# A modulation product moved ahead, a norm's chain put at another priority, and four loads on another queue, in a two-block fp32 kernel

## The chip, the cores and the metric

One Trainium2 chip, one core of it. The metric is the device time of one execution in microseconds (us); before the change three runs gave 2356.71, 2358.75 and 2363.08, median 2358.75. TensorE is called PE, VectorE DVE, ScalarE ACT, GpSimd POOL and the queue of SyncE SP.

## The reference, cut to what matters

Two transformer-like blocks run one after the other on 256 tokens of width 2048, all in fp32.

```python
mod = silu_c @ w_mod[l] + b_mod[l]                       # 2048 -> 6 x 2048
sh1, sc1, g1, sh2, sc2, g2 = split(mod, 6)
hx = modulate(rms_norm(x, norm1_g[l]), sh1, sc1)         # h*(1+scale)+shift
out_x, _, _ = token_mixer(hx, ...)                       # w_in, a scan over tokens, w_pa, w_pb, w_o
x = x + g1 * out_x
h = modulate(rms_norm(x, norm2_g[l]), sh2, sc2)          # the second norm
a, b = split(h @ w_up, 2)
x = x + g2 * ((silu(dwconv_grid(a, dw, db)) * b) @ w_down)   # 3x3 depthwise convolution
# second block: norm, w_in_2, two kinds of attention (one with a per-head norm and rotary
# embedding of q and k, and a norm of its output), gates, w_out_2
```

## The kernel before, in words

Every large product is made on PE in three fp32r parts. A weight block (`blocks`, L138 on) is 512 KB: a DMA on SP's queue into `raw`, ACT makes its rounded part `whi` (L156), DVE the rest `wlo = raw - whi` (L157), and PE uses both. `raw`, `whi` and `wlo` have four buffers each, so the chain SP, ACT, DVE runs up to four blocks ahead of PE. 680 blocks go through it: w_in (from 0), w_pb and w_pa between, w_o (block 224), w_up (256), w_down (320), w_up, w_down, w_up, w_down, w_in_2 (520), w_out_2 (648).

The other work is written as generators. `pump()` (L100) is called after each block and advances the list `bg` (convolution, scans, attention) by one or more yields, and `late`, the generator `late_mod`, by `late_rate` steps. `late_mod` (L655) computes the four parts of `mod` that are needed late: 16 groups of 512 columns, 8 steps each; a step loads 512 KB of w_mod by POOL's queue (L663) into a tile `lm` and adds its two rows of weights to a sum with two DVE instructions (L697; the first of a group L700). With 0.42 steps per pump it ends in the middle of the up-projections.

A scheduler then orders the instructions of each engine by priority, which is the order of writing; what stands under `high_priority(offset=400)` (`AHEAD`, as L156 and L157 do) goes ahead of up to 400 others. Each engine runs its list strictly in order. An instruction in `keep_in_program_order` (`pin`) keeps its place as written.

Around the second norm: `rest` ends with w_o in four column groups; `add_rows` (L1097) adds gate times product to `x`, ACT squares it (L1095), and the last lines make `r2`, the factor of each token. `ffn` scales `x` by `r2` on ACT (L1115), transposes it on PE (L265), and ACT (L1125) and DVE (L1126, L1128) modulate and split it. `x` is loaded by SP's queue in four DMAs of 512 KB just ahead of w_o (L1068). `up(n)` makes 512 columns of a, then of b; `conv` takes 3 of 4 channel groups' taps on DVE (L1166) and the fourth on POOL (L1160, L1162). In the second block `qk_norm` (L1515) and `diff` (L1615) multiply by factors that POOL's queue copies to all partitions (L336), in two pinned halves.

Of the kernel before, what the change touches and what calls it, by code (L numbers as in the profile page):

```python
# [9 lines left out]
AF = mybir.ActivationFunctionType  # L10
ALU = mybir.AluOpType

D = 2048
# [4 lines left out]
EPS = 1e-6  # L18
AHEAD = 400
# [59 lines left out]
class Build:  # L79
    def __init__(self, tc, nc, I, out):  # L80
        self.tc, self.nc, self.I, self.out = tc, nc, I, out
        self.bg = []
        self.late = None
        self.late_rate = 0.42
        self.late_due = 0.0
        self.n_mod = 0
        self.n_name = 0
        self.n_raw = 4
        self.ready = set()
        self.early_cols = (1024, 2048, 2560)  # L90
# [434 lines left out]
        nc.vector.tensor_tensor(out=B, in0=res[1], in1=col(V_BMOD + k0), op=ALU.add)  # L525
        out += [A, B]

    def load_rows(self, ap, i, h):
        t = self.t4((128, 1024))
        self.nc.sync.dma_start(out=t, in_=ap[i * 128:(i + 1) * 128, h * 1024:(h + 1) * 1024])  # L530
        return t

    def norm1(self):
# [434 lines left out]
    def rest(self):  # L968
        nc, v = self.nc, self.vec
        W = self.I["w_in"][0]  # L970
        ax = [self.act(0, i * 128, i * 128 + 128) for i in range(2)]
        tt, stt = nc.vector.tensor_tensor, nc.vector.scalar_tensor_tensor

        def product(c0, out=None, func=AF.Copy):
            banks = self.gemm_tf(W, 0, 16, c0, ax)
            out = self.t4((128, 2, 512))
            for i in range(2):
                nc.scalar.activation(out=out[:, i, :], in_=banks[i], func=func)
            if func is AF.Sigmoid and self.bg:
                self.exp_ln()  # L980
            return out, banks

        def times(banks, o):
            for i in range(2):
                tt(out=o[:, i, :], in0=banks[i], in1=o[:, i, :], op=ALU.mult)

        def conv(g, x, cv):
            u = self.t4((128, 4, 258))
            nc.gpsimd.memset(u[:, :, 0:258:257], 0.0)
            yield  # L990

# [24 lines left out]
        for g in range(2):  # L1016
            x, _ = product(6144 + 512 * g)
            times(self.gemm_tf(W, 0, 16, 7168 + 512 * g, ax), x)
            cv = self.t4()
            self.bg.insert(0, conv(g, x, cv))  # L1020
            x, _ = product(5120 + 512 * g)
            yb.append(self.hl())
            self.bg.insert(0, branch(x, cv, yb[-1]))
        ayb = self.halves(yb)
        mb = []
        for n in range(4):
            sg, _ = product(10240 + 512 * n, func=AF.Sigmoid)
            times(self.gemm_tf(self.I["w_pb"][0], 0, 8, 512 * n, ayb), sg)
            mb.append(sg)

        def attn(sg, g, y):
            on = self.on[g]
            yield

            def fn(b, ps):
                o = on[:, 2 * b:2 * b + 2, :]
                stt(out=o, in0=o, scalar=v[:, V_AN:V_AN + 1], in1=ps, op0=ALU.mult, op1=ALU.mult)
                self.parts(o, y[b])

            yield from self.turned(lambda i: sg[:, i, :], fn)  # L1040
            self.ready.add(y[0].name)

        ya = []
        for g in range(2):
            sg, banks = product(4096 + 512 * g, func=AF.Sigmoid)
            times(banks, sg)
            ya.append(self.hl())
            self.bg.append(attn(sg, g, ya[-1]))
        aya = self.halves(ya)

        def merge(x, y):
            yield
            yield

            def fn(b, ps):
                self.parts(ps, y[b])

            yield from self.turned(lambda i: x[:, i, :], fn)
            self.ready.add(y[0].name)

        mg = []
        for n in range(4):
            sg, _ = product(8192 + 512 * n, func=AF.Sigmoid)
            times(self.gemm_tf(self.I["w_pa"][0], 0, 8, 512 * n, aya), sg)
            tt(out=sg, in0=sg, in1=mb[n], op=ALU.add)
            mg.append(self.hl())
            self.bg.append(merge(sg, mg[-1]))
        self.x = [[self.load_rows(self.I["x"][0], i, h) for h in range(2)] for i in range(2)]  # L1068
        amg = self.halves(mg)
        while self.n_mod < 8:  # L1070
            self.pump()

        self.A2 = self.pc.tile([128, 16], F32, name="A2")
        nc.vector.tensor_scalar(out=self.A2, in0=self.mod[:, 16:32], scalar1=1.0, scalar2=None, op0=ALU.add)
        nc.vector.tensor_tensor(out=self.A2, in0=self.A2, in1=v[:, V_N2:V_N2 + 16], op=ALU.mult)
        ss = self.s1((128, 2, 4))
        for n in range(4):
            banks = self.gemm_tf(self.I["w_o"][0], 0, 16, 512 * n, amg)
            if n == 3:
                self.tc.keep_in_program_order(nc.scalar.preload_act_table_set("natural_log_exp_and_others"))  # L1080
            while self.n_mod < 9 + n:
                self.pump()
            self.add_rows(n, banks, self.gate_rows[0])
            for i in range(2):
                self.squares(self.chunk(i, n), ss[:, i, n:n + 1])
        tot = self.s1((128, 2))
        nc.vector.tensor_reduce(out=tot, in_=ss, axis=mybir.AxisListType.X, op=ALU.add)
        self.r2 = self.s1((128, 2))
        self.rsqrt_mean(self.r2, tot, D, EPS)

    def chunk(self, i, n):
        return self.x[i][n // 2][:, (n % 2) * 512:(n % 2) * 512 + 512]
# [1 line left out]
    def squares(self, x, out):  # L1094
        self.nc.scalar.activation(out=self.t2(), in_=x, func=AF.Square, accum_out=out)  # L1095

    def add_rows(self, n, banks, rows):  # L1097

        nc = self.nc
        r = rows[n // 2][:, (n % 2) * 512:(n % 2) * 512 + 512]  # L1100
        for i, b in enumerate(banks):
            t, x = self.t2(), self.chunk(i, n)
            nc.vector.tensor_tensor(out=t, in0=b, in1=r, op=ALU.mult)
            nc.vector.tensor_tensor(out=x, in0=x, in1=t, op=ALU.add)

    def ffn(self):
        nc, v = self.nc, self.vec
        stt = nc.vector.scalar_tensor_tensor
        hs = [self.hl() for _ in range(4)]

        def normed():
            for n in range(4):
                xs = self.t4((128, 2, 512))
                for i in range(2):
                    nc.scalar.activation(out=xs[:, i, :], in_=self.chunk(i, n), func=AF.Copy,  # L1115
                                         scale=self.r2[:, i:i + 1])
                hf = self.t4()

                def fn(b, ps):
# [16 lines left out]
        n_made = [0]  # L1136

        def wait(k):
            while n_made[0] < min(4, k // 4 + 2):
                next(made, None)  # L1140
                n_made[0] += 1

# [40 lines left out]
        def up(n):  # L1183
            W = self.I["w_up"][0]
            acc = self.t4()
            pads = []
# [12 lines left out]

            self.gemm_wide(W, 0, 16, 512 * n, ah, take, at_once=2 if n else 4, n_pump=1 + n // 8)  # L1200
            y, b = self.hl(), []
            self.bg.append(conv(n, acc, pads, b, y))
            b.append(self.gemm_wide(W, 0, 16, FF + 512 * n, ah, n_pump=2))
            return y

        def down(n0, ys, last):
# [289 lines left out]
    def qk_norm(self, x, wcol, t0):  # L1496

        nc = self.nc
        n = x.shape[2]
# [13 lines left out]
        for i in range(2):  # L1513
            h = slice(2 * i, 2 * i + 2)
            self.pin(nc.vector.scalar_tensor_tensor(out=x[:, h, :], in0=x[:, h, :], scalar=w, in1=rb[:, h, :],  # L1515
                                                    op0=ALU.mult, op1=ALU.mult))
            yield

        for b in (0, 64):
            nc.gpsimd.dma_start(out=rot[b:b + 8], in_=x[b + 8:b + 16])  # L1520
# [18 lines left out]
    def diff(self, g, q, k, vv, do):  # L1539

        nc = self.nc
# [71 lines left out]
        for i in range(2):  # L1613
            h = slice(2 * i, 2 * i + 2)
            self.pin(nc.vector.tensor_tensor(out=do[:, h, :], in0=do[:, h, :], in1=rb[:, h, :], op=ALU.mult))  # L1615
            yield


_INS = [
# [22 lines left out]
```

## Time and profile before

| | |
|---|---|
| median of three runs | 2358.75 us |
| profiled execution, its own time | 2357.4 us |
| its span in the trace | 2355.7 us |
| PE busy, DVE, ACT, POOL | 2279.4 (97%), 1677.1 (71%), 1103.2 (47%), 377.0 us (16%) |
| DMA | 476.19 MB, mean 202 GB/s |
| mean granted PE clock | 0.992 of full speed |

Busy time says how long an engine had an instruction; a line of the waits says which engine stood idle, for whom and how long. Times in stretches are counted from the start of the span.

### The profile page before, as it was taken

The page shows a single profiled execution, that of the slowest core. Times are in us where ns is not written, and L with a number is a line of the kernel's source. Part 1 is how long each engine was busy: PE and PEld are TensorE (multiplying, and loading weights), DVE is VectorE, ACT ScalarE, POOL GpSimd, SP SyncE. Part 2 cuts the span into 40 slices and gives each one's busy share as a digit, 9 for nine tenths or more (in the row PEclk, how much of TensorE's full clock was granted, in tenths as well). Part 3 has the DMA queues.
Part 4 walks back from the last instruction along what each step waited for, and adds up shares of the span by engine and source line. Part 5 has one row for each costly group of instructions (what it writes and reads, how often), then busy time and mean ns, then how long its engine had stood idle before and what let it go on. Part 6 is the DMA issues. An engine that isn't in the chain of part 4 may idle for free. (4 is left out here: it accounts for less than half of the span.)

```text
span 2355.7 us, 33863 instructions
## 1 busy us (share of the span) xinstructions
PE 2279.4 (97%) x12872; PEld 1933.8 (82%) x12872; DVE 1677.1 (71%) x2445; ACT 1103.2 (47%) x1514; POOL 377.0 (16%) x630
## 2 busy tenths in 40 slices
PE   5999999999999999989989999999999999999999
PEld 3689898888888787878777888888888988888887
DVE  3556488788988876888997688757877665653564
ACT  3324344544555543454443445434555463554543
POOL 0200000100001101003540043202220212211000
PEclk9999999999999999999999999999999999999999
DMA  9774443777778778757666666655655657664454
GB/s 317 270 246 158 136 125 120 248 232 240 241 231 269 242 254 315 241 180 232 216 228 214 192 187 184 195 193 186 196 194 183 177 153 162 167 151 126 132 196 155
DMA packets 293123, 476.19 MB, mean 202 GB/s; under 512 B 16153, under 2 KB 151816, under 8 KB 292960
## 3 DMA queue, kind: packets, MB, share of 16 engines
q1 hardware_dynamic: 267120, 387.50, 51.5%
q0 software_dynamic: 25168, 85.50, 12.6%
q8 instruction: 101, 1.65, 0.3%
q10 hardware_dynamic: 672, 1.03, 0.1%
q14 instruction: 62, 0.51, 0.1%
HBM read 468.05 MB, written 2.10 MB: 200 GB/s over the span
## 5 line engine op out<-in xcount | busy, mean ns | idle before, releaser
L156 ACT ACTIVATE whi<-raw 128x1024 fp32r<-128x1024 f32 x680 | 715.7, 1058 | 885.5 <-PE ps L241 399.4
L157 DVE TENSOR_TENSOR wlo<-raw,whi 128x1024 fp32r<-128x1024 f32 x680 | 840.4, 1242 | 364.2 <-ACT whi L156 360.1
L296 PE MATMUL ps<-t,whi 128*128 128x512 f32 (+2 forms) x4096 | 813.4, 343 | 9.1 <-ACT whi L156 5.7
L296 PEld LDWEIGHTS ps<-t,whi 128*128 128x128 f32 x4096 | 633.8, 190 | 108.0 <-issue 26.4
L239 PE MATMUL ps<-whi,t 128*128 128x512 f32 x1376 | 545.3, 396 | 4.2 <-ACT whi L156 4.2
L240 PE MATMUL ps<-wlo,t 128*128 128x512 f32 x1376 | 538.3, 391 | 1.9 <-DVE wlo L157 1.9
L241 PE MATMUL ps<-whi,t 128*128 128x512 f32 x1376 | 538.0, 391 | 0.0
L296 PE MATMUL ps<-t,wlo 128*128 128x256 f32 (+1 forms) x3072 | 441.6, 284 | 18.2 <-DVE wlo L157 18.2
L296 PEld LDWEIGHTS ps<-t,wlo 128*128 128x128 f32 x3072 | 416.2, 190 | 46.6 <-DVE wlo L157 24.1
L239 PEld LDWEIGHTS ps<-whi,t 128*128 128x128 f32 x1376 | 259.4, 189 | 58.8 <-ACT whi L156 4.6
L240 PEld LDWEIGHTS ps<-wlo,t 128*128 128x128 f32 x1376 | 259.5, 189 | 55.3 <-DVE wlo L157 2.7
L241 PEld LDWEIGHTS ps<-whi,t 128*128 128x128 f32 x1376 | 259.3, 188 | 54.2
L663 POOL DMA_DIRECT2D lm<-in_w_mod x128 | 92.8, 725 | 692.7 <-DVE t L697 352.8
L697 DVE SCALAR_TENSOR_TENSOR t<-lm,silc,t 128x512 f32<-128x512 f32 x240 | 180.5, 752 | 5.2 <-DMA lm<-in_w_mod 3.0
L1160 POOL TENSOR_SCALAR cb<-pad,vec 128x256 f32<-128x256 f32 x88 | 84.7, 977 | 430.3 <-DVE pad L211 430.3
L1166 DVE SCALAR_TENSOR_TENSOR t<-pad,vec,t 128x256 f32<-128x256 f32 x264 | 143.6, 573 | 4.3 <-ACT t L1196 2.5
L1162 POOL TENSOR_TENSOR t<-t,cb 128x256 f32<-128x256 f32 x88 | 84.5, 961 | 3.0
L649 DVE TENSOR_TENSOR t<-ps,t 128x256 f32<-128x256 f32 x96 | 36.1, 418 | 57.7 <-PE ps L296 57.6
L296 PE MATMUL ps<-t,t 128*128 128x128 f32 (+5 forms) x352 | 59.1, 332 | 0.8 <-ACT t L1590 0.6
L296 PE MATMUL ps<-em,cstat 128*32 128x512 f32 (+1 forms) x320 | 44.5, 555 | 14.7 <-DVE t L303 11.4
L296 PEld LDWEIGHTS ps<-t,t 128*128 128x128 f32 (+3 forms) x352 | 44.9, 185 | 11.7 <-issue 3.8
L882 ACT ACTIVATE t<-t 128x1024 f32<-128x1024 f32 x28 | 29.6, 1057 | 41.4 <-DVE t L880 36.8
(278 smaller groups left out, 1373.9 us busy)
## 6 DMA issues: line engine op xcount, KB each, us to landing
raw<-in_w_in SPq DMA_DIRECT2D x299, 512.0 KB, 4.1
raw<-in_w_up SPq DMA_DIRECT2D x176, 512.0 KB, 4.0
lm<-in_w_mod POOLq DMA_DIRECT2D x128, 512.0 KB, 5.5
raw<-in_w_down SPq DMA_DIRECT2D x88, 512.0 KB, 3.7
em<-in_w_mod SPq DMA_DIRECT2D x64, 512.0 KB, 6.2
raw<-in_w_o SPq DMA_DIRECT2D x32, 512.0 KB, 4.3
raw<-in_w_out SPq DMA_DIRECT2D x32, 512.0 KB, 3.6
raw<-in_w_in POOLq DMA_DIRECT2D x21, 512.0 KB, 5.8
```

The source lines that it names most:

```text
L156: a = nc.scalar.activation(out=hi, in_=raw, func=AF.Copy)
L157: b = nc.vector.tensor_tensor(out=lo, in0=raw, in1=hi.bitcast(F32), op=ALU.subtract)
L239: nc.tensor.matmul(b, lhsT=ah(kt + k), rhs=hi[:, k, :], start=first, stop=False)
L240: nc.tensor.matmul(b, lhsT=ah(kt + k), rhs=lo[:, k, :], start=False, stop=False)
L241: nc.tensor.matmul(b, lhsT=al(kt + k), rhs=hi[:, k, :], start=False, stop=last)
L296: self.nc.tensor.matmul(o, lhsT=l, rhs=r, start=start, stop=stop, skip_group_check=True)
L649: nc.vector.tensor_tensor(out=e, in0=o, in1=e, op=ALU.add)
L663: nc.gpsimd.dma_start(out=raw, in_=W[kb * 256:kb * 256 + 256, 2 * D + b * 512:2 * D + b * 512 + 512].rearrange("(k p) f -> p k f", p=128))
L697: nc.vector.scalar_tensor_tensor(out=acc, in0=raw[:, j, :], scalar=s, in1=acc, op0=ALU.mult, op1=ALU.add)
L1160: nc.gpsimd.tensor_scalar(out=cb, in0=tap(j, t), scalar1=wt(t, 4 * n + j), scalar2=1.0, op0=ALU.mult, op1=ALU.mult)
L1162: nc.gpsimd.tensor_tensor(out=a, in0=a, in1=cb, op=ALU.add)
L1166: stt(out=a, in0=tap(j, t), scalar=wt(t, 4 * n + j), in1=a, op0=ALU.mult, op1=ALU.add)
```

## The change

`late_rate` is 0.8 until `rest` begins and 0.45 from there. The four loads of `x` go to POOL's queue, one after each of four column groups ahead of w_o. The last column group of w_o is added, squared and reduced under high priority, one half of the tokens after the other. The scaling by `r2` is written ahead of everything else of `ffn`: the first of four chunks half by DVE and half by ACT, at high priority, the other three by POOL. `wait` asks for a normed chunk two k-tiles ahead of its use instead of four. For n below 8 the convolution of `up(n)` is appended to `bg` after b's product instead of ahead of it. In `qk_norm` and `diff` the second pinned half follows five and eight yields after the first instead of one.

```diff
-        self.late_rate = 0.42
+        self.late_rate = 0.8
...
     def rest(self):
+        self.late_rate = 0.45
...
+            self.x[n % 2][n // 2] = self.load_rows(self.I["x"][0], n % 2, n // 2, nc.gpsimd)
-        self.x = [[self.load_rows(self.I["x"][0], i, h) for h in range(2)] for i in range(2)]
...
-            self.add_rows(n, banks, self.gate_rows[0])
-            for i in range(2):
+            if n < 3:
+                self.add_rows(n, banks, self.gate_rows[0])
+                for i in range(2):
+                    self.squares(self.chunk(i, n), ss[:, i, n:n + 1])
+        with self.tc.high_priority(offset=AHEAD):
+            for i in range(2):
+                self.add_rows(n, banks, self.gate_rows[0], (i,))
                 self.squares(self.chunk(i, n), ss[:, i, n:n + 1])
+            nc.vector.tensor_reduce(out=tot, in_=ss, axis=mybir.AxisListType.X, op=ALU.add)
+            self.rsqrt_mean(self.r2, tot, D, EPS)
...
+                if n:
+                    nc.gpsimd.tensor_scalar(out=xs[:, i, :], in0=self.chunk(i, n), scalar1=r, scalar2=1.0,
+                                            op0=ALU.mult, op1=ALU.mult)
+                elif i:
+                    with self.tc.high_priority(offset=AHEAD):
+                        nc.scalar.activation(out=xs[:, i, :], in_=self.chunk(i, n), func=AF.Copy, scale=r)
+                else:
+                    with self.tc.high_priority(offset=AHEAD):
+                        nc.vector.tensor_scalar(out=xs[:, i, :], in0=self.chunk(i, n), scalar1=r, scalar2=None,
+                                                op0=ALU.mult)
...
-            while n_made[0] < min(4, k // 4 + 2):
+            while n_made[0] < min(4, (k + 2) // 4 + 1):
...
-            self.bg.append(conv(n, acc, pads, b, y))
+            work = conv(n, acc, pads, b, y)
+            if n >= 8:
+                self.bg.append(work)
             b.append(self.gemm_wide(W, 0, 16, FF + 512 * n, ah, n_pump=2))
+            if n < 8:
+                self.bg.append(work)
...
-            yield
+            for _ in range(5 - 4 * i):     # qk_norm
+                yield
...
-            yield
+            for _ in range(8 - 7 * i):     # diff
+                yield
```

What DVE does between two weight blocks early in the third up-projection, before and then now (`lm` is a step's load of w_mod, `pad` a plane of the convolution, `ps` a result of PE; lines of the new code are some 20 higher, so that L1186 is the old L1166):

```order
L157 TENSOR_TENSOR wlo_10357<-raw_10354,whi_10356 128x1024
L697 SCALAR_TENSOR_TENSOR t_1706_10032<-lm_10145,silc,t_1706_10032 128x512
L683 TENSOR_TENSOR t_1643_9659<-ps_10235,t_1643_9659 128x512
L697 SCALAR_TENSOR_TENSOR t_1706_10032<-lm_10231,silc,t_1706_10032 128x512
L1166 SCALAR_TENSOR_TENSOR t_1712_10067<-pad_10171,vec,t_1712_10067 128x256
L157 TENSOR_TENSOR wlo_10386<-raw_10383,whi_10385 128x1024
L697 SCALAR_TENSOR_TENSOR t_1706_10032<-lm_10231,silc,t_1706_10032 128x512
L1166 SCALAR_TENSOR_TENSOR t_1712_10067<-pad_10171,vec,t_1712_10067 128x256
L697 SCALAR_TENSOR_TENSOR t_1706_10032<-lm_10282,silc,t_1706_10032 128x512
```
```order
L157 TENSOR_TENSOR wlo_10368<-raw_10365,whi_10367 128x1024
L1197 TENSOR_TENSOR t_1646_9617<-t_1646_9617,t_1706_9980 128x1024
L1186 SCALAR_TENSOR_TENSOR t_1722_10086<-pad_10208,vec,t_1722_10086 128x256
L157 TENSOR_TENSOR wlo_10393<-raw_10390,whi_10392 128x1024
L1186 SCALAR_TENSOR_TENSOR t_1722_10086<-pad_10208,vec,t_1722_10086 128x256
L1186 SCALAR_TENSOR_TENSOR t_1722_10086<-pad_10215,vec,t_1722_10086 128x256
L1186 SCALAR_TENSOR_TENSOR t_1722_10086<-pad_10208,vec,t_1722_10086 128x256
```

The instructions of `late_mod` no longer stand there. In the whole list of DVE, of its 256 multiply-adds 39 stood ahead of weight block 72 before and 70 do now; 53 stood behind block 256, the first of w_up, and 18 do now; between, 164 and 168.

What DVE does at the second norm, before and now (`wlo` are blocks of w_up made ahead; L1103 and L1104, now L1111 and L1112, are `add_rows`; L1087, now L1096, is the reduction; L683 adds a finished gate sum):

```order
L683 TENSOR_TENSOR t_1463_8698<-ps_8965,t_1463_8698 128x512
L157 TENSOR_TENSOR wlo_9153<-raw_9150,whi_9152 128x1024
L1103 TENSOR_TENSOR t_1517_8968<-ps_8793,t_1463_8698 128x512
L1103 TENSOR_TENSOR t_1518_8971<-ps_8794,t_1463_8698 128x512
L1104 TENSOR_TENSOR t_1372_8248<-t_1372_8248,t_1517_8968 128x512
L1104 TENSOR_TENSOR t_1374_8252<-t_1374_8252,t_1518_8971 128x512
L1087 TENSOR_REDUCE s_1521_8978<-s_1375_8257 128x2
```
```order
L157 TENSOR_TENSOR wlo_9193<-raw_9190,whi_9192 128x1024
L1111 TENSOR_TENSOR t_1542_9052<-ps_8884,t_1285_7763 128x512
L1112 TENSOR_TENSOR t_1348_8078<-t_1348_8078,t_1542_9052 128x512
L1111 TENSOR_TENSOR t_1544_9057<-ps_8885,t_1285_7763 128x512
L157 TENSOR_TENSOR wlo_9215<-raw_9212,whi_9214 128x1024
L1112 TENSOR_TENSOR t_1400_8345<-t_1400_8345,t_1544_9057 128x512
L1096 TENSOR_REDUCE s_1540_9050<-s_1401_8350 128x2
```

The gate sum went to an earlier place, and the weight block now stands inside the chain, ahead of its last addition.

What SP's queue issues at the change from w_pa to w_o, before and now:

```order
L149 DMA raw_8260<-in_w_o 128x2x512
L149 DMA raw_8285<-in_w_o 128x2x512
L530 DMA t_1371_8246<-in_x 128x1024
L530 DMA t_1372_8248<-in_x 128x1024
L530 DMA t_1373_8250<-in_x 128x1024
L530 DMA t_1374_8252<-in_x 128x1024
L149 DMA raw_8303<-in_w_o 128x2x512
```
```order
L149 DMA raw_8322<-in_w_pa 128x2x512
L149 DMA raw_8353<-in_w_o 128x2x512
L149 DMA raw_8375<-in_w_o 128x2x512
L149 DMA raw_8393<-in_w_o 128x2x512
L149 DMA raw_8423<-in_w_o 128x2x512
```

The four loads of `x` now stand in POOL's list, with five to seven other DMAs between each two of them.

## Rows read from the trace of the kernel before

**Rows 1.** Waits, whole span: engine, line waited for, total us, times, longest us

```profile
PE ps L296 <- DVE wlo L157: 18.2, 14, 3.4
...
PE ps L265 <- ACT t L1115: 8.4, 2, 7.2
...
PE ps L239 <- ACT whi L156: 4.2, 1, 4.2
```

**Rows 2.** Windows: stretch, length, busy us (instructions) by engine, PE clock, DMA share, GB/s

```profile
290.00:431.00 141.00, 139.96 (x931) 127.35 (x930) 116.39 (x217) 68.38 (x104) 10.83 (x15) 1.00 0.47 146
431.00:482.00 51.00, 50.57 (x253) 41.96 (x252) 44.98 (x66) 30.27 (x44) 5.16 (x8) 1.00 0.76 230
...
700.00:750.00 50.00, 50.00 (x244) 42.17 (x243) 49.23 (x81) 27.40 (x34) 7.32 (x10) 1.00 0.84 282
...
1035.00:1240.00 205.00, 190.13 (x1051) 161.42 (x1050) 190.91 (x274) 98.27 (x137) 85.59 (x125) 0.99 0.66 213
...
1332.00:1510.00 178.00, 178.00 (x1021) 156.61 (x1020) 146.49 (x206) 89.47 (x121) 61.45 (x106) 1.00 0.60 184
```

**Rows 3.** Waits of PE from 1036 to 1246 us

```profile
PE ps L296 <- DVE wlo L157: 11.8, 11, 2.1
PE ps L296 <- ACT whi L156: 3.0, 2, 1.8
PE ps L240 <- DVE wlo L157: 1.4, 1, 1.4
```

**Rows 4.** Windows of line L697 alone: stretch, length, DVE busy (instructions), clock, DMA, GB/s

```profile
1035.00:1260.00 225.00, 39.36 (x51) 0.98 0.66 216
```

**Rows 5.** Windows in which the granted clock was half, columns as in rows 2

```profile
935.00:941.80 6.80, 5.38 (x12) 3.76 (x12) 4.49 (x5) 2.93 (x3) 0.00 (x0) 0.50 0.99 367
...
1187.50:1190.90 3.40, 3.40 (x12) 2.74 (x11) 2.00 (x4) 0.00 (x0) 3.40 (x17) 0.51 0.88 264
1242.10:1245.50 3.40, 3.28 (x8) 2.60 (x9) 3.40 (x7) 0.00 (x0) 0.00 (x0) 0.51 1.01 380
```

**Rows 6.** DMA issues from 906 to 927 us: count, KB each, median us to landing

```profile
lm<-in_w_mod POOLq DMA_DIRECT2D x11, 512.0 KB, 12.4
raw<-in_w_o SPq DMA_DIRECT2D x6, 512.0 KB, 19.5
t<-in_x SPq DMA_DIRECT2D x4, 512.0 KB, 13.5
```

**Rows 7.** Timeline of DVE, then of PE, at the second norm: start, us, what

```profile
1024.04 0.69 DVE L683 TENSOR_TENSOR t<-ps,t 128x512 f32<-128x512 f32 x1 [1.27 <-PE ps L296]
1024.65 1.22 DVE L157 TENSOR_TENSOR wlo<-raw,whi 128x1024 fp32r<-128x1024 f32 x1
1025.78 1.28 DVE L1103 TENSOR_TENSOR t<-ps,t 128x512 f32<-128x512 f32 x2
...
1029.06 0.16 DVE L1087 TENSOR_REDUCE s<-s 128x2 f32<-128x8 f32 x1 [0.80 <-ACT t L1095]
...
1031.18 2.15 PE L265 MATMUL ps<-cst,t 128*128 128x128 f32 x8 [7.18 <-ACT t L1115]
...
1034.94 2.06 PE L296 MATMUL ps<-t,whi 128*128 128x512 f32 x4
```

**Rows 8.** Timeline of DVE and POOL around 1995 us

```profile
1993.64 2.31 DVE L157 TENSOR_TENSOR wlo<-raw,whi 128x1024 fp32r<-128x1024 f32 x1
...
1993.07 4.05 POOL L1531 TENSOR_TENSOR t<-t,t 128x512 f32<-128x512 f32 x2 [3.17 <-DMA t<-t]
```

**Rows 9.** Line L1160: duration in ns, least, median, most; first and last start

```profile
L1160 POOL TENSOR_SCALAR cb<-pad,vec x88: 468/642/2275, 1064.0 to 1718.1; 128x256 f32<-128x256 f32 x88
```

**Rows 10.** Waits of DVE on the copied factors, whole span; of PE from 1803 to 2265 us

```profile
DVE t L1515 <- DMA t<-t: 29.6, 6, 7.6
...
DVE t L1615 <- DMA t<-t: 22.3, 4, 6.3
...
PE ps L296 <- DVE wlo L157: 6.4, 3, 3.4
```

More of the change, by code (lines that the diff above doesn't have):

```diff
@@ L526, in mod_cols, with load_rows @@
         out += [A, B]
-    def load_rows(self, ap, i, h):
+    def load_rows(self, ap, i, h, queue=None):
         t = self.t4((128, 1024))
-        self.nc.sync.dma_start(out=t, in_=ap[i * 128:(i + 1) * 128, h * 1024:(h + 1) * 1024])
+        (queue or self.nc.sync).dma_start(out=t, in_=ap[i * 128:(i + 1) * 128, h * 1024:(h + 1) * 1024])
         return t
@@ L1061, in rest @@
         mg = []
+        self.x = [[None, None], [None, None]]
         for n in range(4):
@@ L1065, in rest @@
             tt(out=sg, in0=sg, in1=mb[n], op=ALU.add)
+            mb[n] = None
             mg.append(self.hl())
             self.bg.append(merge(sg, mg[-1]))
-        self.x = [[self.load_rows(self.I["x"][0], i, h) for h in range(2)] for i in range(2)]
+            self.x[n % 2][n // 2] = self.load_rows(self.I["x"][0], n % 2, n // 2, nc.gpsimd)
         amg = self.halves(mg)
@@ L1082, in rest @@
                 self.pump()
-            self.add_rows(n, banks, self.gate_rows[0])
+            if n < 3:
+                self.add_rows(n, banks, self.gate_rows[0])
+                for i in range(2):
+                    self.squares(self.chunk(i, n), ss[:, i, n:n + 1])
+        tot = self.s1((128, 2))
+        self.r2 = self.s1((128, 2))
+        with self.tc.high_priority(offset=AHEAD):
             for i in range(2):
+                self.add_rows(n, banks, self.gate_rows[0], (i,))
                 self.squares(self.chunk(i, n), ss[:, i, n:n + 1])
[L1086 to L1089, printed above, removed]
+            nc.vector.tensor_reduce(out=tot, in_=ss, axis=mybir.AxisListType.X, op=ALU.add)
+            self.rsqrt_mean(self.r2, tot, D, EPS)
     def chunk(self, i, n):
@@ L1095, in squares, with add_rows @@
         self.nc.scalar.activation(out=self.t2(), in_=x, func=AF.Square, accum_out=out)
-    def add_rows(self, n, banks, rows):
+    def add_rows(self, n, banks, rows, which=(0, 1)):
         nc = self.nc
         r = rows[n // 2][:, (n % 2) * 512:(n % 2) * 512 + 512]
-        for i, b in enumerate(banks):
+        for i in which:
             t, x = self.t2(), self.chunk(i, n)
-            nc.vector.tensor_tensor(out=t, in0=b, in1=r, op=ALU.mult)
+            nc.vector.tensor_tensor(out=t, in0=banks[i], in1=r, op=ALU.mult)
             nc.vector.tensor_tensor(out=x, in0=x, in1=t, op=ALU.add)
@@ L1109, in ffn @@
         hs = [self.hl() for _ in range(4)]
+        scaled = [self.t4((128, 2, 512)) for _ in range(4)]
+        for n, xs in enumerate(scaled):
+            for i in range(2):
+                r = self.r2[:, i:i + 1]
+                if n:
[8 more added lines that the diff above has]
+                                                op0=ALU.mult)
         def normed():
             for n in range(4):
-                xs = self.t4((128, 2, 512))
-                for i in range(2):
-                    nc.scalar.activation(out=xs[:, i, :], in_=self.chunk(i, n), func=AF.Copy,
-                                         scale=self.r2[:, i:i + 1])
+                xs = scaled[n]
                 hf = self.t4()
```

## The prediction, made before the result

> **What bounds the kernel now.** PE is busy for 97% of the span, so time can only be won where it stands idle or runs at half clock. I read the waits of PE first [rows 1]. Apart from the start of the program they are three things: DVE late with the small part of a weight block (18.2 us), the scaled rows of the second norm (8.4 us) and one block's large part at w_o (4.2 us). The windows by stage then say where the first one lies. The first four up-projections (1035 to 1240 us) and the next four (1332 to 1510 us) do the same products; the first take 205 us, with DVE busy for 190.9 us of them, the second 178 us with DVE at 146.5 us and PE never idle [rows 2]. PE's idle time in the first is 11.8 us for DVE and 3.0 us for ACT, with 1.4 us more at the first down-projection [rows 3]. What the first four have and the next four lack is the modulation: L697 runs 51 times there and takes 39.4 us of DVE [rows 4]. So that stage is bound by DVE, with the modulation as the surplus. Last, the windows of half clock: after three of the longer stalls the granted clock is 1.2 instead of 2.4 GHz for 6.8, 3.4 and 3.4 us [rows 5], so that such a stall costs more than its own length.
>
> **The modulation earlier: where it leaves.** By the order, 53 of its instructions stand behind the first block of w_up before, and 18 now. 35 leave; at 39.36 / 51 = 0.77 us [rows 4] this is 27 us of DVE, off a stage where it has 205 - 191 = 14 us free. What is left, 164 us in 205, is the 80% of the undisturbed stage (146.5 of 178: 82%) in which PE does not wait [rows 2]. Won: the idle 11.8 + 3.0 + 1.4 = 16.2 us [rows 3], and half of PE's 3.4 and 3.3 busy us at half clock [rows 5], 3.3 us; together 19.5 us. The ACT waits count too: blocks are late there because the loads of w_mod come in bursts, and those go as well. I leave 1 us for the 18 instructions that remain: 18.5 us. Bounds: 6 us if DVE's order at the convolution is at fault rather than its sum, and 27 us, the whole difference 205 - 178.
>
> **Where it arrives.** 31 more of them stand ahead of weight block 72, at 0.77 us some 24 us of DVE, all of it put into 290 to 482 us. There DVE is busy for 116.4 + 45.0 = 161.4 of 192 us; with 24 us more it is 185 us, 97%. The rows say two things about such a share: from 700 to 750 us DVE is at 98% and PE never idle, from 1035 to 1240 us it is at 93% and PE loses 14.9 us in 205 [rows 2]. What decides is whether DVE's sum exceeds PE's time anywhere for longer than the weight blocks made ahead last. Bounds: 0, and 14.9 x 192 / 205 = 14 us. I take 3 us, nearer to the first row, since the list here is filled by a scheduler and has 7 us left over; and DMA, at 47% to 76% there [rows 2], can take twice the loads of w_mod. In the stage between (0.45 against 0.42) four instructions more are 3 us of DVE in 550: nothing. In the first product of w_up a load of w_mod now stands behind six POOL instructions; DVE may meet it late once: 0.5 us.
>
> **The loads of x.** Between 906 and 927 us eleven loads of w_mod, six blocks of w_o and four loads of x are under way at once, and a block takes 19.5 us to land [rows 6]. PE waits 4.2 us [rows 1] and then works 5.4 us at half clock [rows 5], 2.7 us lost: 6.9 us. Without x the two megabytes at 367 GB/s [rows 5] are 5.7 us of transfers less ahead of the block, more than the 4.2 us by which it was late; the last of the four loads still falls into the burst (1.4 us). I take 6.5 us; bounds 2 and 6.9 us. Two megabytes on POOL's queue delay the loads of w_mod behind them by no more than their own time, and those land long ahead of use.
>
> **The norm's chain.** PE's last work ahead of it ends at 1024.0 us, where DVE begins L683; the first product of w_up starts at 1034.94 [rows 7], 10.9 us later. Now the gate sum is made earlier, and from the last product on: L1111, L1112, L1111 at 0.64 us each (1.28 for two), a weight block of 1.13 us that has crept into the chain, L1112 0.64: 3.7 us; the square, as before 0.8 us; from the reduction to the first transpose 2.1 us (1029.06 to 1031.18), which is the factor and one scaling; four transposes, half of the 2.15 us for eight, 1.1 us; and modulation and split 1.6 us (the eight transposes end at 1033.3). Together 9.3 us, where before PE waited once more for the second scaling on ACT. Won 1.6 us. The half clock stays, since PE still stands idle for 6.6 us.
>
> POOL's scaling is not in the trace. Its nearest row is L1160, 128x256 in 0.642 us (0.47 to 2.28) [rows 9], so 1.3 us for 128x512 and 4.6 us at most. The second chunk's transposes stand behind the first four products, some 4 us after the factor; POOL has the chunk after 2.6 us, at the worst after 9.2 us, which would cost 5 us and more for each of three chunks, some 11 us. I take the median, no wait. But the first split (L1148) and the weight blocks run beside POOL's instructions. In [rows 8] a block's subtraction takes 2.31 us, with a POOL addition of 2 us beside it, against 1.22 us alone [rows 7]: DVE waited 1.1 us. One such meeting can fall into the chain; I count a third of it, 0.4 us, which leaves 1.2 us won; bounds -11 and 4 us. The Trainium skill, SBUF — State Buffer, section "Who interferes with whom", says that a DVE instruction with two SBUF inputs and a GpSimd instruction that reads SBUF shut each other out for a whole instruction; the trace agrees (2.31 against 1.22 us), and if the first split meets POOL's scaling every time, the rule takes 1.3 of the 1.6 us.
>
> **The second block.** DVE stands in its order for the copied factors, 29.6 us at L1515 and 22.3 us at L1615; of that only 6.4 us reach PE as late blocks [rows 10]. Half of the halves now come two or three blocks later, when their copies have landed. The first halves wait as before. I count 3.5 us won; bounds -42 (below) and 7 us. The attention's work ends some eight blocks later, still ahead of its use by the gates in the order.
>
> **The sum.** 18.5 - 3 - 0.5 + 6.5 + 1.2 + 3.5 = 26.2 us. From the profiled execution's 2357.4 us, which has 1.7 us around its span and lies 1.35 us below the median of the three runs: 2331 us; from that median it would be 2332.
>
> **The rivals.**
> - DVE is full early. The moved work is paid where it arrives: 14 us instead of 3, with the first half of 290 to 482 us in the role of 1035 to 1240. For it: 97%. Against it: the row at 98%. 2342 us, 15%.
> - The up-projections stay bound. What delays a block there may be the convolution that stands between two of them, not the sum: 6 us won instead of 18.5. For it: DVE's order still has up to five taps between blocks. Against it: 1332 to 1510 us has the same and no idle PE. 2343.5 us, 10%.
> - All of it. Nothing is lost early, and 7 us won in the second block, 4 at the norm: 2357.4 - 19.5 - 6.9 - 4 - 7 = 2320 us. For it: loads at half of their share early. Against it: the first halves still wait. 12%.
> - Slower: the waits for the copies reach PE. DVE's 29.6 + 22.3 = 51.9 us of waits are hidden now by blocks made ahead; of these PE has paid 6.4 us, and 45.5 are covered [rows 10]. Moved to places where PE needs only 2.8 us for a block (178 us for 64), the cover is shorter. If none is left: 2331 + 3.5 + 45.5 = 2380 us; it is slower than before from 23 us on, half of the cover. For it: first halves still wait up to 7.6 us each. Against it: half of the waiters come later, to landed data. 5%.
> - The change gains nothing: the first two together with half of the gain at x, 2331 + 11 + 12.5 + 3 = 2357 us. 3%.
>
> **How the numbers follow.** The forecast has 55%, with a range of its own of 2323 to 2341 us. The lower end of the whole range takes in most of the better case, the upper both partial ones with some of each other: 2318 to 2350 us. About 7 us (0.3%) is what a measurement can tell, so faster is below 2351.7 us. The first three rivals and the forecast are faster, 92%; from their upper tails I take 4 points: 88% faster, 7% the same, 5% slower.
>
> **What would show it.** Right: up(0) to up(3) in about 187 us with hardly a wait of PE for L157; L697 ends within the second up-projection; w_o starts without a wait and without half clock; the first product of w_up 9.3 us after the last of w_o; the idle of PE from 290 to 482 us a few us. Wrong: DVE waits in the up-projections as before, or the idle of PE moved to 290 to 482 us, or the waits of PE from 1803 us on grown.

## The result and the profile after

The changed kernel takes 2321.26 us (median of four runs, 2320.02 to 2321.47) against 2359.03 us of the kernel before beside it: a ratio of 0.9837, 95% interval 0.982 to 0.9854. The profiled execution took 2321.47 us, its span 2319.7 us, the mean granted clock is 0.995. It is faster, by 10 us more than forecast: below the forecast's own range, 2323 to 2341 us, and inside the whole range, 2318 to 2350 us, which reached down for the better case. It lies where the rival "All of it" put its time, but that is luck: the rival has nothing lost early, where 2.5 us are lost, and 7 us won in the second block, where 13.4 us are.

The stages, each from its first product on PE to the first of the next:

| stage, us | before | after | won | predicted |
|---|---|---|---|---|
| products of w_in, 275 to 357 us | 80.6 | 83.1 | -2.5 | -3 |
| rest, w_o, second norm | 591.0 | 582.5 | 8.5 | 6.5 + 1.2 |
| first four up-projections | 205.5 | 193.6 | 11.9 | 18.5 - 0.5, with the next row |
| first down-projection | 91.2 | 87.1 | 4.1 | |
| w_in_2 and attention | 461.7 | 448.3 | 13.4 | 3.5 |

The other stages differ by under 1 us each. The waits of PE in the whole span, as in [rows 1] (engine, line waited for, total us, times, longest us), the two largest behind the start of the program:

```profile
PE ps L265 <- DVE t L1131: 6.0, 1, 6.0
PE ps L296 <- DVE wlo L157: 4.3, 2, 3.8
```

The late small parts fell from 18.2 us to 4.3 us, and the wait at w_o is gone. What is left of L157 is, but for 0.5 us, one stall of 3.8 us. Two windows of the changed kernel answer to [rows 2] (columns as there). The third is a stretch at half clock; the three of [rows 5] are gone, and this one is new:

```profile
290.00:482.00 192.00, 189.64 (x1175) 167.95 (x1174) 175.65 (x308) 97.82 (x151) 23.99 (x34) 1.00 0.64 200
...
1028.20:1221.80 193.60, 189.08 (x1053) 164.28 (x1054) 176.05 (x250) 95.08 (x133) 74.60 (x129) 0.97 0.60 191
...
1086.50:1093.30 6.80, 6.12 (x20) 5.35 (x21) 6.80 (x11) 1.06 (x1) 0.00 (x0) 0.50 0.53 164
```

From 290 to 482 us DVE went up by 14 us to 91% of the stretch, and PE stands idle for 2.4 us (1.5 us before). In the up-projections 4.5 us of idle PE remain. The timeline of the changed kernel shows the longest stall (start us, length us, engine, line, operation, and in brackets the idle time before it and what ended it):

```profile
1074.34 1.55 POOL L1182 TENSOR_TENSOR t<-t,cb 128x256 f32<-128x256 f32 x1
...
1076.50 0.76 POOL L663 DMA_DIRECT2D lm<-in_w_mod  x1
...
1082.38 0.75 DVE L697 SCALAR_TENSOR_TENSOR t<-lm,silc,t 128x512 f32<-128x512 f32 x1 [7.09 <-DMA lm<-in_w_mod]
...
1085.91 1.22 DVE L157 TENSOR_TENSOR wlo<-raw,whi 128x1024 fp32r<-128x1024 f32 x1
...
1087.18 2.07 PE L296 MATMUL ps<-t,wlo 128*128 128x256 f32 x8 [3.78 <-DVE wlo L157]
```

A load of w_mod stands in POOL's list behind the taps of the first convolution and is issued at 1076.50 us. DVE stands 7.09 us for it, PE 3.78 us, and 6.8 us at half clock follow. This isn't the load that the prediction priced at 0.5 us. That one stands behind six instructions of POOL, the scalings of the norm; it goes out with two others at 1029.23 us (below), and DVE doesn't wait for it.

The norm's chain, for [rows 7]:

```profile
1018.85 0.68 DVE L1111 TENSOR_TENSOR t<-ps,t 128x512 f32<-128x512 f32 x1
1018.90 0.39 PE L241 MATMUL ps<-whi,t 128*128 128x512 f32 x1
...
1020.78 1.22 DVE L157 TENSOR_TENSOR wlo<-raw,whi 128x1024 fp32r<-128x1024 f32 x1
...
1023.38 0.16 DVE L1096 TENSOR_REDUCE s<-s 128x2 f32<-128x8 f32 x1 [0.79 <-ACT t L1103]
...
1024.73 0.49 DVE L1131 TENSOR_SCALAR t<-t,s 128x512 f32<-128x512 f32 x1
1024.80 4.48 POOL L1124 TENSOR_SCALAR t<-t,s 128x512 f32<-128x512 f32 x6 [83.37 <-DVE s L309]
1025.27 1.99 PE L265 MATMUL ps<-cst,t 128*128 128x128 f32 x8 [5.98 <-DVE t L1131]
...
1028.20 1.19 PE L296 MATMUL ps<-t,whi 128*128 128x512 f32 x2 [0.94 <-DVE t L1148]
...
1029.23 2.21 POOL L663 DMA_DIRECT2D lm<-in_w_mod  x3
```

From L1111 to the first product it is 9.35 us, as worked out. From the end of the last product of w_o, at 1019.29 us, it is 8.9 us, where it was 10.9 us before from PE's last work. POOL's six scalings take 4.48 us, 0.75 us each, under the estimate of 1.3 us. POOL had stood still for 83.37 us ahead of them, with everything behind them in its list waiting too: three loads of w_mod go out at 1029.23 us.

### The profile page after: what moved, and what is told of

Its sections match the earlier page's. It is cut to its first block, busy times and chain, and to the rows that moved or that the text cites. A ratio compares the mean times of both kernels' runs of the same rounds, so it can differ in the third digit from the quotient of the medians.

```text
span 2319.7 us, 33903 instructions
## 1 busy us (share of the span) xinstructions
PE 2270.2 (98%) x12872; PEld 1933.9 (83%) x12872; DVE 1687.4 (73%) x2446; ACT 1103.3 (48%) x1509; POOL 378.3 (16%) x640
## 3 DMA queue, kind: packets, MB, share of 16 engines
q1 hardware_dynamic: 266544, 385.40, 51.9%
q0 software_dynamic: 25744, 87.60, 13.4%
## 4 chain that ended last, share of the span: by engine, by line
PE 89%; DMA 3%; DVE 3%; issue 2%; POOL 1%; ACT 1%; SPq 0%; POOLq 0%; DVEq 0%; ACTq 0%
PE ps L296 49%; PE ps L239 13%; PE ps L241 13%; PE ps L240 13%; DVE wlo L157 1%; DMA raw<-in_w_in 1%; DMA raw<-in_w_o 1%; PE ps L265 1%; ACT whi L156 1%; DMA lm<-in_w_mod 0%; DMA em<-in_w_mod 0%; SPq L495 0%; POOL cb L1180 0%; POOL t L1182 0%; DMA t<-in_b_mod 0%
## 5 line engine op out<-in xcount | busy, mean ns | idle before, releaser
L157 DVE TENSOR_TENSOR wlo<-raw,whi 128x1024 fp32r<-128x1024 f32 x680 | 844.2, 1247 | 353.5 <-ACT whi L156 352.1
L697 DVE SCALAR_TENSOR_TENSOR t<-lm,silc,t 128x512 f32<-128x512 f32 x240 | 180.6, 753 | 10.7 <-DMA lm<-in_w_mod 8.2
L1186 DVE SCALAR_TENSOR_TENSOR t<-pad,vec,t 128x256 f32<-128x256 f32 x264 | 147.0, 593 | 5.3 <-ACT t L1216 3.5
L1180 POOL TENSOR_SCALAR cb<-pad,vec 128x256 f32<-128x256 f32 x88 | 78.1, 901 | 432.0 <-DVE pad L211 432.0
```

Source lines behind the costliest of these rows:

```text
L157: b = nc.vector.tensor_tensor(out=lo, in0=raw, in1=hi.bitcast(F32), op=ALU.subtract)
L697: nc.vector.scalar_tensor_tensor(out=acc, in0=raw[:, j, :], scalar=s, in1=acc, op0=ALU.mult, op1=ALU.add)
L1180: nc.gpsimd.tensor_scalar(out=cb, in0=tap(j, t), scalar1=wt(t, 4 * n + j), scalar2=1.0, op0=ALU.mult, op1=ALU.mult)
L1186: stt(out=a, in0=tap(j, t), scalar=wt(t, 4 * n + j), in1=a, op0=ALU.mult, op1=ALU.add)
```

## The experiments

### Each part alone, on the kernel before

```diff
-        self.late_rate = 0.42          # e1_late
+        self.late_rate = 0.8
...
+        self.late_rate = 0.45          # first line of rest()
```

> The kernel before with late_rate alone changed (0.8, then 0.45 from rest on). Theory (the modulation's share of DVE was the surplus of the up-projections): PE's time from the first product of w_up to the first of w_down falls from 205.5 to about 194 us and the first down-projection from 91.2 to about 87 us, while the stage from 275 to 444 us grows by about 3 us: together 13 us, 2346 us. With it a stall of about 4 us near the first up-projection, where the last four loads of w_mod stand in POOL's list behind the convolution's taps. Rival (the place of the convolution, not DVE's sum, held the blocks up): the up-projections stay above 200 us, and the whole is 2353 us or more.

Measured: 2342.15 us, ratio 0.9928 (0.9913 to 0.9943). First up-projections 191.5 us, first down-projection 87.1 us: 18.1 us won there, where the prediction has 18.5; the products from 275 to 358 us take 83.3 us, 2.7 us lost. So the theory holds, in size too. (In the six profiles without this edit the first up-projections take 205.2 to 208.2 us.) Two things came out otherwise. The whole is 4 us faster than expected, and the stall of about 4 us did not come: the load of w_mod stands behind 15 instructions of taps here too, but DVE comes to it so late that it hardly waits:

```profile
1083.19 0.78 POOL L663 DMA_DIRECT2D lm<-in_w_mod  x1
...
1091.35 0.75 DVE L697 SCALAR_TENSOR_TENSOR t<-lm,silc,t 128x512 f32<-128x512 f32 x1 [0.23 <-DMA lm<-in_w_mod]
```

```diff
+            self.x[n % 2][n // 2] = self.load_rows(self.I["x"][0], n % 2, n // 2, nc.gpsimd)   # e2_x
-        self.x = [[self.load_rows(self.I["x"][0], i, h) for h in range(2)] for i in range(2)]
```

> The kernel before with only the four loads of x moved to POOL's queue. Theory (the two megabytes on SP's queue delayed the blocks of w_o): no wait of PE at the start of w_o, no half clock there, 7 us less: 2352 us. Rival (the burst of loads of w_mod alone delays the block): a wait of 2 us or more stays and with it the half clock; 2357 us.

Measured: 2351.58 us, ratio 0.9969 (0.9958 to 0.9981); the stage up to the norm goes from 591.0 to 583.1 us, with neither a wait of PE nor half clock at w_o.

```diff
+        with self.tc.high_priority(offset=AHEAD):      # e3_norm: add_rows by halves, reduction
+                    nc.gpsimd.tensor_scalar(out=xs[:, i, :], in0=self.chunk(i, n), ...)
-            while n_made[0] < min(4, k // 4 + 2):
+            while n_made[0] < min(4, (k + 2) // 4 + 1):
```

> The kernel before with only the second norm's part: last column group of w_o by halves at high priority, scaling by DVE and ACT and for three chunks by POOL, chunks asked for later. Theory: from the last product of w_o to the first of w_up 9 to 9.5 us instead of 10.9 (12.2 with the gate sum that stands between), 1.5 us won, 2357.5 us. Rival (POOL's scaling shuts DVE out of its first splits): 0 us or slower, with DVE's L1148 over 0.8 us there.

Measured: 2359.04 us, ratio 1.0004 (0.9994 to 1.0013): nothing won. Its timeline shows why:

```profile
1021.39 1.02 PE L296 MATMUL ps<-t,ones 128*128 128x512 f32 x2
1029.61 1.99 PE L265 MATMUL ps<-cst,t 128*128 128x128 f32 x8 [7.20 <-DVE t L1128]
1033.25 3.33 PE L296 MATMUL ps<-t,whi 128*128 128x512 f32 x7 [1.66 <-DVE t L1145]
```

The product with ones, the gate sum of the modulation, still ends w_o at 1022.41 us, and from there to the first product it is 10.8 us, as before. The rival's number came without its reason: the first split (L1145 here) takes 0.42 us, not over 0.8 us. In e1_late, which has the gate sum earlier and nothing of the norm's part, the chain from the last product of w_o (1027.73 us) to the first of w_up (1037.57 us) takes 9.8 us. So of the 2.0 us by which it got shorter in the changed kernel, 10.9 to 8.9 us, 1.1 us come from the gate sum's earlier place, which the prediction counted together with the norm's own edit.

```diff
+            for _ in range(5 - 4 * i):      # e4_yields: qk_norm (e5_qk: this alone)
+            for _ in range(8 - 7 * i):      # diff (e6_diff: this alone)
```

> The kernel before with only the yields between the pinned halves (5 in qk_norm, 8 in diff). In the whole change the second block, from the first product of w_in_2 to the first of w_out_2, fell from 461.7 to 448.3 us, 13.4 us, where 3.5 were forecast. Theory (the pairs of waits back to back were what broke through the blocks made ahead): all of it comes from here, 2345.5 us. Rival (the rest of the change shifted the loads and so the waits against PE): 3 to 5 us, 2354 us or more.

Measured: 2344.0 us, ratio 0.9933 (0.9917 to 0.995). The stage of w_in_2 takes 448.3 us, exactly that of the whole change: all of its 13.4 us come from the yields. (It takes 461.1 to 462.9 us in the four profiles without the yields, 448.3 to 449.3 us in the eight with both.)

### Which of the two pairs of halves

> The kernel before, with one edit: the second half of the two scaled halves in qk_norm yields five times instead of once ahead of the first half's... that is, the halves stand further apart in DVE's order; the halves in diff stay as they were. Both edits together won 14.5 us (2344.0), nearly all of it in the stage of w_in_2 (461.7 to 448.3 us). Theory A, each edit wins the stalls of PE that stand behind its own waits: behind qk_norm's copies PE waits 0.7 + 3.4 + 1.6 us between 1987 and 2032 us and has some busy time around them, so 7 to 9 us here: 2350 to 2352, and the stage at 453 to 455 us. Rival B, one place in DVE's order delays all that follows it, and the first pair of halves is that place: then this edit wins either nearly all (2345) or nearly nothing (2357), and the other one the rest.

> The kernel before, with one edit: the halves in diff stand further apart (eight yields instead of one), those in qk_norm as they were. Theory A: behind diff's copies PE waits 2.4 us at 1963 us and 1.2 us at 2101 us, so 4 to 6 us are won: 2353 to 2355, the stage of w_in_2 at 456 to 458 us, and the sum of this gain and the one of qk_norm alone is the 14.5 us of both. Rival B: nearly all (2345) or nearly nothing (2357). Rival C, the two only work together: each wins under 4 us alone.

Measured: 2353.22 us, ratio 0.9984 (0.9974 to 0.9993), and 2352.49 us, 0.9975 (0.9965 to 0.9984). The stage goes from 461.7 to 456.8 us by the one and to 454.1 us by the other: 4.9 + 7.6 = 12.5 of the 13.4 us. Theory A holds in kind; its split, 7 to 9 and 4 to 6, was the wrong way round. That the two add up rests on the stages: by the times they win 4.9 + 5.6 = 10.5 of 14.5 us, each with an interval of some 2 us either way, and in e6_diff's profile the first up-projections, where its edit does nothing, took 2.7 us longer than before. The waits of PE from 1780 to 2242 us, in the kernel with qk_norm's yields, then in the one with diff's, then with both:

```profile
PE ps L296 <- DVE wlo L157: 5.2, 3, 2.7
...
```

```profile
PE ps L296 <- ACT t L1590: 2.3, 2, 1.7
PE ps L296 <- DVE wlo L157: 1.9, 1, 1.9
```

```profile
PE ps L296 <- DVE t L1244: 1.0, 1, 1.0
PE ps L296 <- ACT t L1591: 1.0, 2, 0.6
PE ps L296 <- ACT whi L156: 0.6, 1, 0.6
PE ps L296 <- POOL t L1419: 0.2, 1, 0.2
```

With both no wait for a small part is left.

### The stall at 1087 us

```diff
-        self.late_rate = 0.45          # f1_rate052, in rest() of the changed kernel
+        self.late_rate = 0.52
```

> The changed kernel, with the modulation's rate in the rest stage 0.52 instead of 0.45, so that its last instruction stands ahead of w_up. Theory: the 3.8 us that PE waits at 1087 us, and the 6.8 us at half clock that follow (3.4 us lost), come from one load of w_mod that stands in GpSimd's order behind the convolution's taps; with no load left there both go, and up(0) to up(3) take 186 to 188 us instead of 193.6: 2313 to 2316 us. Rival, the stall comes from DVE's sum in the first two up-projections: the instructions taken away there are few, and DVE has 10 us more work ahead, at 290 to 1020 us: 2319 to 2324 us, with new waits of PE in the rest stage.

Measured: 2312.86 us, ratio to before 0.9807 (0.9791 to 0.9823), 8.4 us below the change. The stall and its half clock are gone, and in the window of the up-projections PE is never idle:

```profile
1030.10:1213.00 182.90, 182.90 (x1049) 161.07 (x1050) 164.23 (x229) 94.82 (x132) 59.94 (x107) 0.99 0.56 173
```

This run takes DVE's instructions away as well as the loads. The next ones part the two.

```diff
-            if n >= 8:                 # f2_noconv, up() of the changed kernel
-                self.bg.append(work)
+            self.bg.append(work)
             b.append(self.gemm_wide(W, 0, 16, FF + 512 * n, ah, n_pump=2))
-            if n < 8:
-                self.bg.append(work)
```

> The changed kernel with the convolutions appended in the order of before (no difference between the first eight and the others). Theory: the order of the convolutions' work only moves DVE's and GpSimd's instructions by a product or so and DVE is no longer full there, so up(0) to up(3) change by under 2 us: 2319 to 2324. Rival: GpSimd's taps are what the load of w_mod stands behind, and with the old order they come at another time, so that the wait of 3.8 us at 1087 us goes: 2313 to 2316, or it falls on a block earlier and is longer: 2325 to 2330.

Measured: 2321.01 us, ratio 0.9842 (0.9826 to 0.9858). The time is the theory's, but not by its reason: the 3.8 us stall is gone, and PE waits elsewhere from 1030 to 1222 us:

```profile
PE ps L296 <- DVE wlo L157: 2.6, 3, 1.6
PE ps L296 <- ACT whi L156: 2.3, 1, 2.3
```

The convolutions' order moves stalls about and wins nothing by itself.

```diff
-            nc.gpsimd.dma_start(       # g1_sp_loads, late_mod of the changed kernel
+            (nc.sync if b == 15 else nc.gpsimd).dma_start(
```

> The changed kernel, with the loads of the modulation's last block (eight of the 128) issued by SP's queue instead of GpSimd's; the modulation's instructions on DVE stay where they are. Theory, the stall at 1087 us comes from the load that GpSimd issues only after its convolution taps: the wait of 3.8 us and the half clock behind it go though DVE has the same work, up(0) to up(3) take 184 to 188 us instead of 193.6, the whole 2313 to 2316 us. Rival, DVE's sum in the first two up-projections is too large: the block is late all the same, 2319 to 2323 us. Rival 2, SP holds the load back behind its own wait for a free buffer of a weight block: up to 10 us of a wait on DVE, 2321 to 2330 us.

Measured: 2320.4 us, ratio 0.9837 (0.9822 to 0.9852): the stall stays, 3.2 us at the same place. But the waits of DVE from 1030 to 1222 us name another transfer:

```profile
DVE t L683 <- DMA t<-in_b_mod: 6.3, 1, 6.3
```

It is the row of b_mod that goes with the same gate. POOL still issues it, behind the same taps, as POOL's timeline of this kernel shows:

```profile
1073.13 0.88 POOL L1182 TENSOR_TENSOR t<-t,cb 128x256 f32<-128x256 f32 x1
...
1074.42 0.59 POOL L289 DMA_DIRECT2D t<-in_b_mod  x1
```

So the run fell on the first rival's number without its reason. A kernel with this row on SP's queue too was not tried.

```diff
-        scaled = [self.t4((128, 2, 512)) for _ in range(4)]     # g2_no_norm_part: the norm's
-                    nc.gpsimd.tensor_scalar(out=xs[:, i, :], ...)   # part of the change undone
+                    nc.scalar.activation(out=xs[:, i, :], in_=self.chunk(i, n), func=AF.Copy, ...)
```

> The changed kernel without its part on the norm: scaling by ACT alone, chunk after chunk, the gate sum and reduction at ordinary priority, the wait rule of before. Alone, on the kernel before, this part won nothing (2359.0 to 2358.5). Theory A, the parts do not act on one another: 2320 to 2323 us, and from the last product of w_o to the first of w_up about 11 us. Theory B, the part needs the others (x landed early, DVE less full): 2324 to 2328 us, a loss of 3 us and more where it is left out. Theory C, the part even costs, since GpSimd's scaling takes DVE's port and its place in GpSimd's order delays the load: 2313 to 2318 us, the stall at 1087 us gone.

Measured: 2315.75 us, ratio 0.9818 (0.9803 to 0.9832): theory C. Without its part on the norm the change is 5.5 us faster. The up-projections take 187.8 instead of 193.6 us with as much work on DVE (177.2 us busy against 176.1), so it isn't DVE's sum. POOL's list has no scaling that waits for the factor, and the loads leave early:

```profile
982.67 0.72 POOL L663 DMA_DIRECT2D lm<-in_w_mod  x1 [41.61 <-DVE t L697]
...
1057.93 0.54 POOL L1163 TENSOR_SCALAR cb<-pad,vec 128x256 f32<-128x256 f32 x1 [35.45 <-PE ps L296]
1058.45 0.78 POOL L663 DMA_DIRECT2D lm<-in_w_mod  x1
```

The load that was issued at 1076.50 us stands behind one tap here, and the 982.67 us load stood behind the scaling there, at 1029.23 us. The first of these two is the one that PE paid for. How the norm's part moved it behind the other 15 taps, when the scheduler made the list, no run here takes apart. By the Trainium skill, PSUM — Partial Sum Buffer, section "Engine vs sequencer instructions", the queues of ScalarE, VectorE and GpSimd are strictly first in, first out; the trace agrees, with the 83.37 us that POOL stood at its scaling.

### A faster kernel

```diff
-        self.late_rate = 0.8           # h1_rates_065_060: the changed kernel, 0.65 and 0.6
+        self.late_rate = 0.65
...
-        self.late_rate = 0.45
+        self.late_rate = 0.6
```

> The changed kernel with the modulation spread otherwise: rate 0.65 instead of 0.8 up to the rest stage and 0.6 instead of 0.45 in it, so that the last of it stands ahead of w_up as with 0.52, and fewer of it (43 instructions instead of 54) ahead of weight block 72. With 0.8 and 0.52 the time was 2312.9 us, and the stage at 400 to 482 us takes 2.3 us longer than before the change. Theory: this loss comes from the early instructions and goes with a part of them, while the rest stage has room (DVE at 90% there): 2310.5 to 2312.5 us. Rival: DVE has no room for 25 us more from 482 to 900 us, and PE waits there: 2314 to 2322 us.

Measured: 2313.96 us, ratio 0.9812 (0.9796 to 0.9828). That is just under the rival's range and above the theory's. The loss of 2.3 us stands at 275 to 358 us, not at 400 to 482 us as the expectation has it. It shrinks to 1.2 us (81.8 us), and the next products win 1.4 us, but the rest stage takes 588.5 instead of 584.1 us: from 475 to 1019 us PE is idle for 2.45 us, mostly behind L885, where with 0.8 and 0.52 it is never idle; the other 2 us of that stage are not accounted for. So what is won early is lost again there.

The kernel of f1_rate052 and, last, the same without the norm's part (i1_rate052_no_norm_part: the edit of g2_no_norm_part and 0.52 instead of 0.45):

> The changed kernel with the modulation's rate 0.52 in the rest stage and without the part on the norm: both edits that each took the stall at 1087 us away (2312.9 and 2315.8 us). Theory, with no load left behind GpSimd's scaling and taps the part on the norm costs nothing any more and wins what its chain is shorter by (last product of w_o to first of w_up 9.3 against 10.9 us): 2313 to 2316 us, slower than with the part. Rival, the part costs in itself, by GpSimd's scaling beside DVE: the 1.7 us that PE waits for the first split go too, and it is 2309 to 2312 us, the fastest kernel.

Measured: 2312.44 us, ratio 0.981 (0.9797 to 0.9824), no different from 2312.86 us, and between the two expectations: the part neither costs nor wins anything that can be measured here. Stage by stage the part wins 0.3 us up to the norm and 0.8 us behind it, no more than the 0.6 us by which the two profiles differ from 275 to 358 us, where it does nothing. PE at the norm, first with the part, then without:

```profile
1026.41 1.99 PE L265 MATMUL ps<-cst,t 128*128 128x128 f32 x8 [5.63 <-DVE t L1131]
1030.06 3.48 PE L296 MATMUL ps<-t,whi 128*128 128x512 f32 x8 [1.66 <-DVE t L1148]
```

```profile
1027.78 2.15 PE L265 MATMUL ps<-cst,t 128*128 128x128 f32 x8 [5.87 <-ACT t L1118]
...
1031.54 2.06 PE L296 MATMUL ps<-t,whi 128*128 128x512 f32 x4
```

The last products of w_o end at 1020.79 and 1021.92 us, so the chain takes 9.3 us with the part and 9.6 us without. Both kernels are faster than the change; one number, 0.52, does it.

## Why the prediction was right, and where not

- **The modulation leaves: right.** 18.5 us against 18.1 us alone and 11.9 + 4.1 = 16.0 us in the change. Too small was the 1 us left for the 18 instructions that stayed: without them f1_rate052 wins 22.6 us in the up-projections and 4.1 us behind them, 10.7 us more than the change (the late load, below, is part of it) and close to the bound of 27 us.
- **It arrives early: right in size, not in kind.** 3 us against 2.5 us. The rival "DVE is full early" is out: DVE's busy time in that stretch rose by 14 us to 91%, not by 24 us to 97%; seven of the 31 multiply-adds run ahead of 290 us. But PE never waits for a weight block there. From 275 to 357 us it stands idle for 1.5 us, for tiles of the scans (L807, L814, L885).
- **The late load: a step that failed.** I counted one load behind six POOL instructions and 0.5 us; it goes out at 1029.23 us and costs nothing. The load that costs stands behind a whole convolution's 16 instructions of taps, and the sum has no term for it. It cost 5.8 us in the stage (g2_no_norm_part against the change). The taps alone don't cost that: with 15 of them ahead of the load e1_late's DVE waits 0.2 us. It counts where DVE's list asks for the data.
- **The loads of x: right,** 6.5 us against 6.9 us by the time of e2_x and 7.9 us by its stage.
- **The norm's chain: right in length, wrong in cause.** 9.35 us from L1111 where 9.3 us were predicted, but 1.1 of the 2.0 us that the chain lost come from the gate sum's earlier place, which is the modulation's doing. Alone the part wins nothing; with its order on POOL it costs 5.5 us. The 0.4 us set aside for a meeting of the first split with POOL's scaling did not come: L1148 takes 0.44 us at 1027.62 us, amid the scalings, and 0.43 us at 1030.38 us, after them.
- **The second block: this is the step that mis-sized the sum.** Predicted 3.5 us, measured 13.4 us, outside its bound of 7 us too. These 9.9 us are as much as the whole difference between 26.2 and 36 us; the misses of the other terms, from -2.0 to +0.8 us, nearly cancel. I counted only the 6.4 us at L157 [rows 10] and half of those. The windows of the stage, before and after, show what was to be had:

```profile
1806.20:2267.90 461.70, 449.50 (x3008) 397.79 (x3008) 265.76 (x373) 225.99 (x365) 73.23 (x123) 1.00 0.59 155
```

```profile
1783.90:2232.20 448.30, 445.42 (x3008) 396.52 (x3007) 265.54 (x372) 230.12 (x366) 71.21 (x123) 1.00 0.61 160
```

  PE's idle time was 461.7 - 449.5 = 12.2 us and is 2.9 us: 9.3 us won. 6.4 us of them are the wait for weight blocks, all of it and not half; 2.1 us are waits for tiles that DVE makes for the attention (L1346), the rest is behind ACT and POOL. PE's busy time fell by 4.1 us, of which 1.7 us is half of the 3.4 us at half clock (2201 us) that are gone; 2.4 us I cannot name. "The first halves wait as before" was nearly so, yet none of it reaches PE: the waits of DVE for the copies in the changed kernel are

```profile
DVE t L1539 <- DMA t<-t: 21.3, 6, 5.9
DVE t L1640 <- DMA t<-t: 15.2, 3, 5.2
```

  36.5 of 51.9 us. In `diff` it is the second wait close behind the first that hurt PE, before DVE had made blocks ahead again. Before:

```profile
1954.38 0.69 DVE L1615 TENSOR_TENSOR t<-t,t 128x512 f32<-128x512 f32 x1 [6.22 <-DMA t<-t]
1961.38 0.69 DVE L1615 TENSOR_TENSOR t<-t,t 128x512 f32<-128x512 f32 x1 [6.30 <-DMA t<-t]
...
1963.26 1.27 PE L296 MATMUL ps<-t,wlo 128*128 128x272 f32 x8 [2.42 <-DVE wlo L157]
```

  In the changed kernel both halves still wait, with two weight blocks made between them, and PE isn't idle there:

```profile
1938.80 0.69 DVE L1640 TENSOR_TENSOR t<-t,t 128x512 f32<-128x512 f32 x1 [4.97 <-DMA t<-t]
1939.41 2.35 DVE L157 TENSOR_TENSOR wlo<-raw,whi 128x1024 fp32r<-128x1024 f32 x2
1946.92 0.69 DVE L1640 TENSOR_TENSOR t<-t,t 128x512 f32<-128x512 f32 x1 [5.16 <-DMA t<-t]
```

  In `qk_norm` it is another thing. PE's longest stall of the stage stands behind one wait, that of a first half; its second half waited for 0.14 us:

```profile
2016.79 0.79 DVE L1515 SCALAR_TENSOR_TENSOR t<-t,vec,t 128x544 f32<-128x544 f32 x1 [7.55 <-DMA t<-t]
...
2018.77 1.28 PE L296 MATMUL ps<-t,wlo 128*128 128x272 f32 x8 [3.35 <-DVE wlo L157]
```

  This wait is 5.93 us in the changed kernel, and PE doesn't stand for it. Why it got shorter, and what part that has in the gain, is open. Either way the rival in which these waits reach PE had the sign wrong.

Two readings of the prediction are off, without weight in the sum. PE's waits are not three things: those for ACT's large parts ahead of other blocks are 5.7 us, more than the 4.2 us at w_o. And 5 us and more for each of three chunks, POOL's worst case, is over 15 us, not 11 us.

The four parts alone win 16.3 + 6.9 - 0.6 + 14.5 = 37.1 us, and the change 37.8 us. That sum agrees partly by chance, since the norm's part costs 5.5 us in company and nothing clear of noise alone (0.6 us); which pair of the others wins more together is open. The convolutions' order, a fifth part, was not tried alone.

## What to carry to other kernels

Price a stall in a stage by all of the engine's idle time there and the half clock behind it, not by the one line of waits that the edit names: 6.4 us stood in that line, and 13.4 us were won. Before a queue's list gets an instruction that waits for a late value, list what stands behind it, DMA issues above all, and where the engine that uses the data asks for it: six scalings that cost 4.5 us of POOL held a load back by 47 us at no cost, and another load, whose place in the list changed with them, cost 5.8 us. Two waits of over 6 us in a row cost PE 2.4 us here; two of some 5 us with two blocks made between them cost it nothing.

## What the runs showed of the hardware

POOL scales 128x512 fp32 in 0.75 us, hardly more than the 0.64 us for 128x256 [rows 9]. While POOL works through the taps, both engines' instructions stretch, as the timeline of the changed kernel has it:

```profile
1062.25 1.22 DVE L697 SCALAR_TENSOR_TENSOR t<-lm,silc,t 128x512 f32<-128x512 f32 x1
1062.90 1.96 POOL L1180 TENSOR_SCALAR cb<-pad,vec 128x256 f32<-128x256 f32 x1
...
1068.15 0.95 DVE L1186 SCALAR_TENSOR_TENSOR t<-pad,vec,t 128x256 f32<-128x256 f32 x1
```

L1186 takes 0.48 us where POOL is still (1083.04 us), L697 0.75 us (1082.38 us), and L1180 0.64 us at 1068.80 us. It isn't so with every pair: L1148 beside POOL's scalings was not stretched (0.44 us). And the 3.4 us at half clock at 2201 us of the kernel before followed a wait of PE of 0.2 us only; no run here says why.
